# A key search that keeps its trial threshold, in a kernel whose order follows corrected durations

## The chip, the cores and the metric

The kernel runs on one core of a Trainium2 chip. Its engines are TensorE (PE; PEld is its weight load), VectorE (DVE), ScalarE (ACT), GpSimd (POOL) and SyncE (SP, which issues the transfers). The metric is the device time of one execution in microseconds (us). The trace is one profiled execution, which gives the span from the first to the last instruction and the granted TensorE clock.

## The reference

A decoder block on x of 2048 tokens by 1024 channels, in float32. After a norm and one input projection it has two branches. One is a state-space branch (S5, 32 groups of 64 complex states, solved over chunks of 8 tokens). The other is sparse attention: an indexer scores every earlier key for each query, the 256 best are kept, and eight heads attend to those.

```python
rel = jax.nn.relu(jnp.einsum('bqhd,bsd->bqhs', qib, kif))
iscore = jnp.einsum('bqhs,bqh->bqs', rel, wib * w_scale)
iscore = jnp.where(visible[None], iscore, -jnp.inf)
_, idx = lax.top_k(iscore, k_sel)          # k_sel = 256
...
merged = sigmoid(g_ssm) * (y_ssm @ w_proj_ssm) + sigmoid(g_att) * (y_att @ w_proj_attn)
x = x + merged @ w_out
h2 = rms(x)
x = x + (silu(h2 @ w_ffn_gate) * (h2 @ w_ffn_up)) @ w_ffn_down
```

Matrix products are done as three products of a high and a low part (`mm3`), so PE carries most of the work.

## The kernel before

**Streams.** After phase 1 (norm, input projection) three streams of work share the engines: `state` (the state-space branch), `attention` (the indexer's top-k and then the attention, in four rounds of four query tiles of 128), and `dense` (gates, then four blocks of 512 tokens: merge, output projection, norm, FFN). Block `tb` starts when the attention of its tiles is done (`attended >= 4 * (tb + 1)`), so the top-k and attention of a round run beside the dense block of the round before.

**The plan.** Each stream is a Python generator. While the program is built, `Pace` books every instruction on a model of its engine (`note`: a price from operation, size and type; the time when the engine, `free`, and the data, `done`, are ready). `among` and `pick` take the first stream whose next step could start by the time the model gives for PE; a step that waits on `idle("DVE")` may come when DVE's booked time is no more than `AHEAD` past PE's (2.5 us, 7 in the dense blocks). `spare` chooses by these prices between POOL, DVE and ACT for side work. The result is a fixed order on each engine's queue; at run time an engine takes its instructions in that order.

**The top-k.** `topk` (method of `Block`) first writes the scores of a tile into `S[i]` (128 queries by (i+1) x 128 keys), then `search` finds, for every query, the bits of the 256th largest score, from bit 30 to bit 0, counting in each step how many scores lie beyond a trial threshold. A round has two tiles searched alone as "wide" groups (one column of state each; the count is a Sign activation on ACT, `jka`) and one "narrow" group of two tiles (two columns; the counts are compare-and-add passes on DVE, `jkd`). A narrow group searches the upper 16 bits on `H`, the upper halves as bf16; at bit 15 it rebuilds `H` as 16-bit numbers and searches the lower 16 in float32, with `tf` as the trial and `kf` as the part found. The first round has one wide and one narrow group of one tile each, its tiles 0 and 1 needing no search. The searches of a round run as streams beside each other.

**A step before.** `b` holds the key found so far and `tr` the trial. When the count `cnt` is there, DVE does three one- or two-column operations: `acc = cnt <= threshold`, a predicated copy of `tr` into `b` where `acc` holds, and `tr = b xor bit`:

```python
nc.vector.tensor_tensor(acc, cnt, thr if wide and bit < 30 else thd, op=ALU.is_le)
nc.vector.copy_predicated(cur, acc, tf if low and bit < 15 else tr)
if not low:
    nc.vector.tensor_scalar(tr, b, 1 << bit, None, op0=ALU.bitwise_xor)
```

In the lower half of a narrow group the same three work on `kf` and `tf`, with an addition in the place of the xor. Then come the counts with the new trial. After the last bit the ties are settled and a bias tile (`fin`) is stored for the attention.

**Names in the rows.** All rows show line 199, the helper through which each instruction is recorded, so tiles tell them apart. `f` is a PSUM bank of the dense blocks; `act`, `ww`, `mg` are the merge's inputs, weights and result; the products `f<-ww,mg` (256 columns) are the output projection, `x<-f,x` its and the FFN's residual additions, `ss`, `rr`, `ha` the norm behind it; `f<-h,ww` and `f<-wd,at` are the FFN's up and down products, `t` and `at` what stands between them. `lg`, `pt`, `po` belong to the attention.

Of the kernel before, what the change touches and what calls it, by code (L numbers as in the profile page):

```python
# [12 lines left out]
F32 = mybir.dt.float32  # L13
F32R = mybir.dt.float32r
BF16 = mybir.dt.bfloat16
I32 = mybir.dt.int32
U16 = mybir.dt.uint16
AF = mybir.ActivationFunctionType
ALU = mybir.AluOpType
# [13 lines left out]
TOPK = 256  # L33
# [18 lines left out]
class Pace:  # L52
# [4 lines left out]
    TABLES = {AF.Exp: ("exp",), AF.Tanh: ("exp", "silu"), AF.Silu: ("silu",)}  # L57
    RATE = {"DVE": (1.05e-3, 0.07), "ACT": (0.84e-3, 0.06), "POOL": (2.06e-3, 0.07)}

# [12 lines left out]
    def note(self, eng, op, args, kw):  # L72
        aps = [z for z in (*args, *kw.values()) if isinstance(z, bass.AP)]
        out = kw.get("out", aps[0])
        names = [self.key(z) for z in aps]
        size = math.prod(out.shape[1:])
        if eng == "PE":
            if op == "transpose":
                cost = size * 0.85e-3
            else:  # L80
                cost = math.prod(aps[2].shape[1:]) * 0.422e-3 * (1 if aps[1].dtype == F32R else 4)
        elif eng == "SP":
            cost = out.shape[0] * size * mybir.dt.size(out.dtype) / 360e3
        else:
# [8 lines left out]
            if "accum_out" in kw:  # L93
                cost += 0.2 if eng == "ACT" else 0.07
            if op == "reciprocal":
                cost += size * 5 * r
            elif eng == "POOL" and "pow" in str(kw.get("op")):
                cost += 0.4 + size * 0.1
            elif eng == "POOL" and op == "memset":
                cost -= size * r * 0.6  # L100
# [258 lines left out]
class Block:  # L359
# [431 lines left out]
    def topk(self, st, groups, KL):  # L791
# [39 lines left out]
        for j, (tiles, wide) in enumerate(groups):  # L831
            for i in tiles:
                S[i] = sp.tile([128, (i + 1) * 128], F32, name=f"S{i}")
                yield from iscore(i, S[i], kis)
            n = len(tiles)
            b = qp.tile([128, n], I32, name=f"b{j}", bufs=1)
            nc.vector.memset(b, -1)
            states.append((tiles, b))
# [4 lines left out]
        def count(x, i, t, c):  # L843

            nc.vector.tensor_scalar(jkd[:, :(i + 1) * 128], x, t, 0.0, op0=ALU.is_lt, op1=ALU.add, accum_out=c)

        def search(j, tiles, b, wide):

            n = len(tiles)
            thr, thd, cnt, kf, tf = (qp.tile([128, n], F32, name=f"{m}{j}", bufs=1)
                                     for m in ("thr", "thd", "cnt", "kf", "tf"))
            tr, acc, top = (qp.tile([128, n], I32, name=f"{m}{j}", bufs=1) for m in ("tr", "acc", "top"))
            for q, i in enumerate(tiles):
                W = (i + 1) * 128
                nc.vector.memset(thd[:, q:q + 1], float(W - TOPK))
                if wide:
                    nc.vector.memset(thr[:, q:q + 1], float(W - 2 * TOPK + 1))  # L860
            t = tr.bitcast(F32)
            nc.vector.tensor_scalar(tr, b, -1, None, op0=ALU.bitwise_xor)
            for q, i in enumerate(tiles):
# [3 lines left out]
            if not wide:  # L867
                X = {}
                for i in tiles:
                    yield idle("DVE")  # L870
                    X[i] = sp.tile([128, (i + 1) * 128], BF16, name=f"H{i}")
                    nc.vector.tensor_copy(X[i], S[i].bitcast(BF16).rearrange("p (w a) -> p w a", a=2)[:, :, 1])

            for bit in range(30, -1, -1):
                if wide:
                    yield idle("DVE", cnt)
                low = not wide and bit < 16
                cur = kf if low and bit < 15 else b
                nc.vector.tensor_tensor(acc, cnt, thr if wide and bit < 30 else thd, op=ALU.is_le)
                nc.vector.copy_predicated(cur, acc, tf if low and bit < 15 else tr)  # L880
                if not low:
                    nc.vector.tensor_scalar(tr, b, 1 << bit, None, op0=ALU.bitwise_xor)
                elif bit == 15:

                    nc.vector.tensor_scalar(top, b, 65535, None, op0=ALU.bitwise_xor)
                    nc.vector.tensor_scalar(kf, b, 0.0, None, op0=ALU.is_ge)
                    sg = qp.tile([128, n], F32, name=f"sgn{j}", bufs=1)
                    of = qp.tile([128, n], F32, name=f"off{j}", bufs=1)
                    nc.vector.tensor_scalar(sg, kf, 2.0, -1.0, op0=ALU.mult, op1=ALU.add)
                    nc.vector.tensor_scalar(of, kf, -65535.0, 65535.0, op0=ALU.mult, op1=ALU.add)  # L890
                    for q, i in enumerate(tiles):
# [11 lines left out]
                        nc.vector.tensor_tensor(X[i], X[i], Z, op=ALU.max)  # L903
                    nc.vector.memset(kf, 0.0)
                    nc.vector.memset(tf, float(1 << bit))
                else:
                    nc.vector.tensor_scalar(tf, kf, float(1 << bit), None, op0=ALU.add)
                for q, i in enumerate(tiles):
# [6 lines left out]
            yield idle("DVE", cnt)  # L915
            nc.vector.tensor_tensor(acc, cnt, thr if wide else thd, op=ALU.is_le)
            nc.vector.copy_predicated(b if wide else kf, acc, tr if wide else tf)
            if not wide:
                nc.vector.tensor_copy(tr, kf)
                nc.vector.tensor_tensor(b, b, tr, op=ALU.bitwise_xor)  # L920
# [1054 lines left out]
```

## Time and profile before

| | |
|---|---|
| median of 3 runs | 3481.62 us (3478.7 to 3488.02) |
| the profiled execution | 3482.83 us, span 3480.7 us |
| mean granted PE clock | 0.963 |
| PE busy | 3187.9 us, 92% |
| DVE busy | 2187.6 us, 63%, 4674 instructions |
| ACT, POOL busy | 1258.2 us (36%), 732.0 us (21%) |

Busy shares are means over stages with different limits; the stretches between 393.8 us (the first trial) and 2565 us alternate between searches and attention. A wait names the engine whose signal came last. Idle time of an engine counts only where it ends in idle time of PE or delays the end. A granted clock of 1.00 is 2.4 GHz, the lower level is half of it.

### The profile page before, as it was taken

What the parts mean: (1) busy time and instruction counts of PE and PEld (TensorE: products, weight loads), DVE (VectorE), ACT (ScalarE), POOL (GpSimd) and SP (SyncE); (2) the same over time, 40 slices, a digit from 0 to 9 for tenths busy, and PEclk for the clock granted to TensorE, in tenths of its full rate; (3) what the DMA queues carried; (4) which work ended last, traced back from release to release, by engine and by line L of the source; (5) the groups of instructions that cost most, each with busy time, mean ns of one, the idle gap of its engine ahead of it and who ended that gap; (6) DMA issues with size and microseconds to landing.
All of it is one profiled execution on the core that took longest, in us unless ns stands there. A gap on an engine that the chain in (4) does not pass through costs nothing. (4 is left out here: it accounts for less than half of the span.)

```text
span 3480.7 us, 44710 instructions
## 1 busy us (share of the span) xinstructions
PE 3187.9 (92%) x16292; PEld 2692.5 (77%) x16292; DVE 2187.6 (63%) x4674; ACT 1258.2 (36%) x2186; POOL 732.0 (21%) x1016
## 2 busy tenths in 40 slices
PE   6999989888978999988879999979699999999999
PEld 5879767766756888766778888758588888798887
DVE  4555675567577566698786775996876666322222
ACT  3141444546532444455212444664124443110000
POOL 3323777762213312244100000001000000000000
PEclk8999999999988999999989999999899999999999
DMA  4833323443448854766845325347363232755544
GB/s 133 247 117 112 123 81 110 134 129 100 146 163 292 283 196 172 254 216 211 305 147 224 124 81 189 148 178 264 127 252 116 95 144 91 274 222 218 193 170 181
DMA packets 321531, 605.70 MB, mean 174 GB/s; under 512 B 52896, under 2 KB 205216, under 8 KB 290592
## 3 DMA queue, kind: packets, MB, share of 16 engines
q1 hardware_dynamic: 321312, 602.86, 49.6%
q8 instruction: 128, 2.10, 0.2%
q14 instruction: 91, 0.75, 0.1%
HBM read 434.71 MB, written 166.89 MB: 173 GB/s over the span
## 5 line engine op out<-in xcount | busy, mean ns | idle before, releaser
L199 PE MATMUL f<-h,ww 128*128 128x512 f32 (+1 forms) x4416 | 1012.5, 383 | 3.3 <-DVE x L199 2.0
L199 PEld LDWEIGHTS f<-h,ww 128*128 128x128 f32 x4416 | 798.2, 189 | 158.5 <-DVE x L199 2.4
L199 PE MATMUL f<-wd,at 128*128 128x512 f32 x2112 | 529.6, 403 | 60.0 <-ACT at L199 37.7
L199 PEld LDWEIGHTS f<-wd,at 128*128 128x128 f32 x2112 | 402.0, 194 | 156.3 <-issue 26.5
L199 PE MATMUL gps<-hT,gw 128*128 128x512 f32 x1536 | 386.9, 402 | 10.3 <-ACT gsg L199 9.8
L199 ACT ACTIVATE jka<-S,tr 128x896 bf16<-128x896 f32 (+6 forms) x217 | 305.6, 1408 | 234.6 <-DVE tr L199 170.2
L199 PEld LDWEIGHTS gps<-hT,gw 128*128 128x128 f32 x1536 | 285.6, 191 | 72.5 <-ACT gsg L199 9.5
L199 DVE TENSOR_TENSOR x<-f,x 128x512 f32<-128x512 f32 x352 | 236.5, 687 | 94.7 <-PE f L199 94.0
L199 PE MATMUL mm<-w,hT 128*128 128x512 f32 (+1 forms) x1152 | 283.4, 404 | 7.3 <-DVE hT L199 7.1
L199 DVE TENSOR_TENSOR tl<-pt,th 128x512 fp32r<-128x512 f32 (+1 forms) x288 | 184.2, 658 | 146.7 <-ACT th L199 145.9
L199 DVE SCALAR_TENSOR_TENSOR t<-t,f 128x512 f32<-128x512 f32 (+1 forms) x127 | 84.4, 665 | 305.2 <-PE f L199 260.7
L199 PEld LDWEIGHTS mm<-w,hT 128*128 128x128 f32 x1152 | 243.4, 241 | 33.2 <-DVE hT L199 8.8
L199 ACT CAST th<-pt 128x512 fp32r<-128x512 f32 (+1 forms) x288 | 155.8, 563 | 234.0 <-PE pt L199 232.1
L199 PE MATMUL f<-act,ww 128*128 128x512 f32 x768 | 188.2, 406 | 34.9 <-DMA act<-act 14.2
L199 POOL TENSOR_TENSOR g<-g,g 128x512 f32<-128x512 f32 x31 | 39.8, 1283 | 856.6 <-issue 553.4
L199 PEld LDWEIGHTS f<-act,ww 128*128 128x128 f32 x768 | 149.4, 197 | 73.3 <-issue 16.5
L199 PE MATMUL f<-ww,mg 128*128 128x256 f32 x1536 | 192.2, 288 | 10.5 <-DMA ww<-wc 4.1
L199 PEld LDWEIGHTS f<-ww,mg 128*128 128x128 f32 x1536 | 190.0, 196 | 13.1 <-issue 5.2
L199 ACT ACTIVATE P<-P,m 128x1024 f32<-128x1024 f32 (+7 forms) x192 | 172.2, 900 | 71.4 <-DVE m L199 71.1
L199 PE MATMUL lg<-kk,q 128*128 128x512 f32 (+1 forms) x640 | 183.2, 388 | 1.4 <-DMA kk<-kk 1.4
L199 ACT CAST at<-t 128x512 fp32r<-128x512 f32 (+1 forms) x92 | 55.2, 600 | 326.3 <-DVE t L199 326.3
L199 ACT ACTIVATE t<-f 128x512 f32<-128x512 f32 (+1 forms) x92 | 52.9, 575 | 310.8 <-PE f L199 310.7
(356 smaller groups left out, 4668.6 us busy)
## 6 DMA issues: line engine op xcount, KB each, us to landing
ww<-wc SPq DMA_DIRECT2D x180, 1024.0 KB, 4.9
wd<-wc SPq DMA_DIRECT2D x66, 1024.0 KB, 8.5
wc<-ww SPq DMA_DIRECT2D x60, 1024.0 KB, 7.4
raw<-in_w_in_dram SPq DMA_DIRECT2D x104, 256.0 KB, 3.3
wc<-wd SPq DMA_DIRECT2D x22, 1024.0 KB, 7.6
x<-in_x_dram SPq DMA_DIRECT2D x32, 512.0 KB, 5.8
gate<-gsg SPq DMA_DIRECT2D x64, 256.0 KB, 2.1
g<-gate SPq DMA_DIRECT2D x64, 256.0 KB, 5.5
```

What stands on the lines that cost most here:

```text
L199: return f(*args, **kw)
```

## The change

The search keeps the trial threshold itself in `tr` (or `tf`) and corrects it after each count. `missed` makes, in one operation, the word to take back: (count misses the target) times twice the bit, an integer in `un` or a negative float in `uf`. A second operation combines it with the trial and the next bit: two xors in one scalar-tensor-tensor instruction, or two additions. The copies, `acc`, `thr`, `thd` and `kf` go, and the memsets that fed them; `b` is made once, at bit 15 or at the end. The narrow count is now of scores at or above the trial instead of below it.

Beside it, prices of the plan change: POOL per element 2.06 to 2.25 ns; a product of PE from 0.422 ns a column to (columns + 32) / 2.4 GHz; a DVE operation with an accumulator 0.14 us more instead of 0.07; DVE operations of at most 8 columns get fixed prices (0.1 us for `tensor_scalar` and memset, 0.25 for a predicated copy, 0.2 for others); DVE operations on fewer than 128 partitions 0.09 more; POOL's power 0.15 us a column instead of 0.1.

```diff
--- before.py
+++ after.py
@@ -55,7 +55,7 @@
     AHEAD, SLACK, BIAS = 2.5, 0.3, 0.0
     TIGHT = 0.5
     TABLES = {AF.Exp: ("exp",), AF.Tanh: ("exp", "silu"), AF.Silu: ("silu",)}
-    RATE = {"DVE": (1.05e-3, 0.07), "ACT": (0.84e-3, 0.06), "POOL": (2.06e-3, 0.07)}
+    RATE = {"DVE": (1.05e-3, 0.07), "ACT": (0.84e-3, 0.06), "POOL": (2.25e-3, 0.07)}
 
     def __init__(self, nc):
         self.free = dict.fromkeys(("PE", "DVE", "ACT", "POOL", "SP"), 0.0)
@@ -78,7 +78,8 @@
             if op == "transpose":
                 cost = size * 0.85e-3
             else:
-                cost = math.prod(aps[2].shape[1:]) * 0.422e-3 * (1 if aps[1].dtype == F32R else 4)
+                n = math.prod(aps[2].shape[1:])
+                cost = (n + 32) / 2.4e3 if aps[1].dtype == F32R else n * 4 / 2.4e3
         elif eng == "SP":
             cost = out.shape[0] * size * mybir.dt.size(out.dtype) / 360e3
         else:
@@ -91,11 +92,17 @@
             elif eng == "DVE" and op in ("tensor_scalar", "tensor_tensor") and short:
                 cost -= size * r / 2
             if "accum_out" in kw:
-                cost += 0.2 if eng == "ACT" else 0.07
+                cost += 0.2 if eng == "ACT" else 0.14
             if op == "reciprocal":
                 cost += size * 5 * r
+            elif eng == "DVE" and size <= 8 and op not in ("tensor_scalar", "memset"):
+                cost = 0.25 if op == "copy_predicated" else 0.2
+            elif eng == "DVE" and size <= 8:
+                cost = 0.1
+            elif eng == "DVE" and out.shape[0] < 128:
+                cost += 0.09
             elif eng == "POOL" and "pow" in str(kw.get("op")):
-                cost += 0.4 + size * 0.1
+                cost += 0.4 + size * 0.15
             elif eng == "POOL" and op == "memset":
                 cost -= size * r * 0.6
             if eng == "ACT" and op == "activation":
@@ -834,7 +841,6 @@
                 yield from iscore(i, S[i], kis)
             n = len(tiles)
             b = qp.tile([128, n], I32, name=f"b{j}", bufs=1)
-            nc.vector.memset(b, -1)
             states.append((tiles, b))
         banks.close()
         self.spare_banks = 4
@@ -842,24 +848,19 @@
 
         def count(x, i, t, c):
 
-            nc.vector.tensor_scalar(jkd[:, :(i + 1) * 128], x, t, 0.0, op0=ALU.is_lt, op1=ALU.add, accum_out=c)
+            nc.vector.tensor_scalar(jkd[:, :(i + 1) * 128], x, t, 0.0, op0=ALU.is_ge, op1=ALU.add, accum_out=c)
 
         def search(j, tiles, b, wide):
 
 
 
 
+
             n = len(tiles)
-            thr, thd, cnt, kf, tf = (qp.tile([128, n], F32, name=f"{m}{j}", bufs=1)
-                                     for m in ("thr", "thd", "cnt", "kf", "tf"))
-            tr, acc, top = (qp.tile([128, n], I32, name=f"{m}{j}", bufs=1) for m in ("tr", "acc", "top"))
-            for q, i in enumerate(tiles):
-                W = (i + 1) * 128
-                nc.vector.memset(thd[:, q:q + 1], float(W - TOPK))
-                if wide:
-                    nc.vector.memset(thr[:, q:q + 1], float(W - 2 * TOPK + 1))
+            cnt, tf, uf = (qp.tile([128, n], F32, name=f"{m}{j}", bufs=1) for m in ("cnt", "tf", "uf"))
+            tr, un, top = (qp.tile([128, n], I32, name=f"{m}{j}", bufs=1) for m in ("tr", "un", "top"))
             t = tr.bitcast(F32)
-            nc.vector.tensor_scalar(tr, b, -1, None, op0=ALU.bitwise_xor)
+            nc.vector.memset(tr, 0)
             for q, i in enumerate(tiles):
                 yield idle("DVE")
                 count(S[i], i, t[:, q:q + 1], cnt[:, q:q + 1])
@@ -871,23 +872,34 @@
                     X[i] = sp.tile([128, (i + 1) * 128], BF16, name=f"H{i}")
                     nc.vector.tensor_copy(X[i], S[i].bitcast(BF16).rearrange("p (w a) -> p w a", a=2)[:, :, 1])
 
+            def missed(out, value, signs):
+
+                if signs:
+                    W = (tiles[0] + 1) * 128
+                    nc.vector.tensor_scalar(out, cnt, float(W - 2 * TOPK + 1), float(value), op0=ALU.is_gt, op1=ALU.mult)
+                else:
+                    nc.vector.tensor_scalar(out, cnt, float(TOPK), float(value), op0=ALU.is_lt, op1=ALU.mult)
+
             for bit in range(30, -1, -1):
                 if wide:
                     yield idle("DVE", cnt)
                 low = not wide and bit < 16
-                cur = kf if low and bit < 15 else b
-                nc.vector.tensor_tensor(acc, cnt, thr if wide and bit < 30 else thd, op=ALU.is_le)
-                nc.vector.copy_predicated(cur, acc, tf if low and bit < 15 else tr)
-                if not low:
-                    nc.vector.tensor_scalar(tr, b, 1 << bit, None, op0=ALU.bitwise_xor)
-                elif bit == 15:
+                if low and bit < 15:
+                    missed(uf, -(2 << bit), False)
+                    nc.vector.scalar_tensor_tensor(tf, uf, float(1 << bit), tf, op0=ALU.add, op1=ALU.add)
+                else:
+                    missed(un, -1 if bit == 30 else 2 << bit, wide and bit < 30)
+                    if not low:
+                        nc.vector.scalar_tensor_tensor(tr, un, 1 << bit, tr, op0=ALU.bitwise_xor, op1=ALU.bitwise_xor)
+                if low and bit == 15:
+                    nc.vector.tensor_tensor(b, tr, un, op=ALU.bitwise_xor)
 
                     nc.vector.tensor_scalar(top, b, 65535, None, op0=ALU.bitwise_xor)
-                    nc.vector.tensor_scalar(kf, b, 0.0, None, op0=ALU.is_ge)
+                    nc.vector.tensor_scalar(uf, b, 0.0, None, op0=ALU.is_ge)
                     sg = qp.tile([128, n], F32, name=f"sgn{j}", bufs=1)
                     of = qp.tile([128, n], F32, name=f"off{j}", bufs=1)
-                    nc.vector.tensor_scalar(sg, kf, 2.0, -1.0, op0=ALU.mult, op1=ALU.add)
-                    nc.vector.tensor_scalar(of, kf, -65535.0, 65535.0, op0=ALU.mult, op1=ALU.add)
+                    nc.vector.tensor_scalar(sg, uf, 2.0, -1.0, op0=ALU.mult, op1=ALU.add)
+                    nc.vector.tensor_scalar(of, uf, -65535.0, 65535.0, op0=ALU.mult, op1=ALU.add)
                     for q, i in enumerate(tiles):
                         c = slice(q, q + 1)
                         yield idle("DVE")
@@ -901,10 +913,7 @@
                         Z = jkd.bitcast(U16)[:, :W]
                         nc.vector.tensor_scalar(Z, S[i], top.bitcast(F32)[:, c], 65535.0, op0=ALU.is_gt, op1=ALU.mult)
                         nc.vector.tensor_tensor(X[i], X[i], Z, op=ALU.max)
-                    nc.vector.memset(kf, 0.0)
                     nc.vector.memset(tf, float(1 << bit))
-                else:
-                    nc.vector.tensor_scalar(tf, kf, float(1 << bit), None, op0=ALU.add)
                 for q, i in enumerate(tiles):
                     if wide:
                         nc.scalar.activation(jka[:, :(i + 1) * 128], S[i], AF.Sign, bias=t[:, q:q + 1], scale=-1.0,
@@ -913,10 +922,12 @@
                         yield idle("DVE")
                         count(X[i], i, (tf if low else t)[:, q:q + 1], cnt[:, q:q + 1])
             yield idle("DVE", cnt)
-            nc.vector.tensor_tensor(acc, cnt, thr if wide else thd, op=ALU.is_le)
-            nc.vector.copy_predicated(b if wide else kf, acc, tr if wide else tf)
-            if not wide:
-                nc.vector.tensor_copy(tr, kf)
+            if wide:
+                missed(un, 1, True)
+                nc.vector.tensor_tensor(b, tr, un, op=ALU.bitwise_xor)
+            else:
+                missed(uf, -1, False)
+                nc.vector.tensor_tensor(tr, tf, uf, op=ALU.add)
                 nc.vector.tensor_tensor(b, b, tr, op=ALU.bitwise_xor)
 
         yield from self.pace.among([search(j, *states[j], groups[j][1]) for j in range(len(groups))])
```

## Rows read from the trace of the kernel before

**Rows 1.** Stretches: us, busy PE, PEld, DVE, ACT, POOL (instructions), clock, DMA.

```profile
760.00:1120.00 360.00, 301.19 (x1488) 247.31 (x1489) 257.92 (x659) 165.86 (x297) 98.89 (x84) 0.92 0.50 163
...
1480.00:1840.00 360.00, 300.76 (x1468) 252.74 (x1467) 303.84 (x629) 134.75 (x185) 95.28 (x52) 0.91 0.62 224
1840.00:2200.00 360.00, 359.47 (x1936) 306.85 (x1935) 241.78 (x496) 154.53 (x292) 1.08 (x3) 1.00 0.38 139
2200.00:2560.00 360.00, 303.03 (x1516) 254.85 (x1516) 303.38 (x626) 163.33 (x185) 13.77 (x13) 0.93 0.52 193
```

**Rows 2.** PE's waits, 1480 to 1840: waiter, releaser, total us, times, longest.

```profile
PE f L199 <- ACT at L199: 24.6, 5, 8.0
PE f L199 <- DVE ss L199: 13.7, 1, 13.7
```

**Rows 3.** PE's waits, 2200 to 2560.

```profile
PE f L199 <- DVE ss L199: 25.1, 1, 25.1
PE f L199 <- ACT at L199: 11.5, 3, 10.2
PE f L199 <- DVE t L199: 10.1, 3, 4.3
```

**Rows 4.** Timeline, DVE and PE: start us, us, instruction [idle before <-releaser].

```profile
2459.78 2.08 DVE L199 TENSOR_SCALAR_CACHE_REDUCE jkd<-H,tf 128x1792 bf16<-128x1792 uint16 x1
...
2462.37 0.68 DVE L199 SCALAR_TENSOR_TENSOR x<-f,x 128x512 f32<-128x512 f32 x1
...
2466.58 1.94 PE L199 MATMUL f<-ident,ha 128*128 128x128 f32 x8 [25.05 <-DVE ss L199]
```

**Rows 5.** PE's waits, 760 to 1120.

```profile
PE f L199 <- DMA act<-act: 14.2, 1, 14.2
```

**Rows 6.** Timeline of DVE, a narrow step and a wide one.

```profile
2403.47 0.16 DVE L199 TENSOR_TENSOR acc<-cnt,thd 128x2 int32<-128x2 f32 x1
...
2404.06 1.95 DVE L199 TENSOR_SCALAR_CACHE_REDUCE jkd<-H,tf 128x1664 bf16<-128x1664 uint16 x1
...
2405.93 0.16 DVE L199 TENSOR_TENSOR acc<-cnt,thr 128x1 int32<-128x1 f32 x1
2406.12 0.22 DVE L199 COPY_PREDICATED_SCALAR b<-acc,tr 128x1 int32 x1
2406.38 0.15 DVE L199 TENSOR_SCALAR tr<-b 128x1 int32<-128x1 int32 x1
2406.45 2.07 DVE L199 TENSOR_SCALAR_CACHE_REDUCE jkd<-H,tf 128x1792 bf16<-128x1792 uint16 x1
```

**Rows 7.** Timeline of DVE, two small operations behind the search.

```profile
2501.76 0.16 DVE L199 TENSOR_TENSOR b<-b,tr 128x2 int32<-128x2 int32 x1
2501.84 2.34 DVE L199 TENSOR_SCALAR_CACHE_REDUCE jkd<-S,b 128x2048 bf16<-128x2048 f32 x1
...
2513.67 0.15 DVE L199 SCALAR_TENSOR_TENSOR r<-ssum,gt 128x1 f32<-128x1 f32 x1
```

**Rows 8.** All instructions on the compare's result: count: ns min/median/max, first and last, forms.

```profile
L199 DVE TENSOR_TENSOR acc<-cnt,thr x217: 146/153/2353, 398.6 to 2442.4; 128x1 int32<-128x1 f32 x109
L199 DVE TENSOR_TENSOR acc<-cnt,thd x135: 147/161/2386, 396.1 to 2501.2; 128x2 int32<-128x2 f32 x96, 128x1 int32<-128x1 f32 x39
```

**Rows 9.** Groups of DVE, 2200 to 2560: busy us, mean ns | idle before.

```profile
L199 DVE TENSOR_SCALAR_CACHE_REDUCE jkd<-H,tf 128x1792 bf16<-128x1792 uint16 x16 | 33.2, 2076 | 0.3
```

**Rows 10.** Timeline of PE, two runs of products.

```profile
2348.50 43.80 PE L199 MATMUL f<-act,ww 128*128 128x512 f32 x192 [1.33 <-DVE x L199]
...
2400.47 20.78 PE L199 MATMUL f<-ww,mg 128*128 128x256 f32 x171 [0.22 <-DVE mg L199]
```

**Rows 11.** DVE's waits, 2200 to 2560.

```profile
DVE mg L199 <- ACT mg L199: 19.9, 8, 3.6
```

**Rows 12.** Timeline, the end of the last attention: PE and the SP queue.

```profile
2971.16 1.11 PE L199 MATMUL lg<-r,hsel 8*128 8x128 f32 x8
...
3004.68 4.27 SPq L199 DMA_DIRECT2D act<-att  x4
```

## The prediction

> **What bounds the kernel now.** I read the table by stage first. TensorE (PE) is busy 92% of the span, so the question is where the other 8% sits. [rows 1] is a table of stretches: in the attention stretch shown, 1840 to 2200, PE has 359.5 of 360 us and a granted clock of 1.00. Nothing can be won there. In the three stretches in which a key search runs it has 301, 301 and 303 of 360 us, at a mean clock of 0.92, 0.91 and 0.93. So each search stretch loses 57 to 59 us of idle PE, and about 0.07 to 0.09 x 360 = 25 to 32 us more because part of it ran at the lower of the two clock levels. That is some 85 us a stretch, 255 us in all, and it is all that this change can reach.
>
> Then the waits of PE in these stretches. In the third and fourth searches they name the dense block's own short chains: `at` and `t` (the gated products of the FFN) and `ss`, the norm's sum [rows 2, 3]. These are cheap operations; what makes them late must be read off VectorE's (DVE's) queue. [rows 4] shows it at the longest wait: PE sits idle 25.05 us before 2466.58, while DVE runs count after count of the search; the last residual addition `x<-f,x` before the norm, 0.68 us of work, comes at 2462.37, behind them, and `ss` only after it. DVE works in the order in which the build-time plan issued, and the plan believed that it would be through earlier. The second search stretch is different: its longest wait, 14.2 us, is for a transfer at the start of the first dense block [rows 5].
>
> **Removed work, by rows.** A wide step (one column) is compare, predicated copy, xor: the compare starts at 2405.93, the xor at 2406.38 and the next DVE instruction at 2406.45, 0.52 us after the compare [rows 6]. A narrow one (two columns) starts at 2403.47 and its count at 2404.06: 0.59. The new step is a compare with multiply, then a scalar-tensor-tensor that depends on it. From a one-column operation to the one that depends on it the row has 0.19 us (compare to copy) [rows 6]; a one-column scalar-tensor-tensor takes 0.15, no longer than a compare, and after a two-column xor of two tensors the next instruction starts 0.08 later [rows 7]. So I take 0.27 for a wide step and 0.39 for a narrow one whose count must wait: 0.25 and 0.20 saved. No row shows an integer scalar-tensor-tensor with two xors. Its bounds are those 0.08 (like the plain xor) and the 0.25 us of the predicated copy (2406.12 to 2406.38); then a wide step saves only 0.07 and a narrow one about 0.03. I take the first, since the operation is nearest to the xor in kind and to the row of [rows 7] in length.
>
> The compares number 217 + 135 = 352 [rows 8], which is 224 wide steps and 128 narrow ones. 224 x 0.25 + 128 x 0.20 = 82 us of DVE, by the other bound 224 x 0.07 + 128 x 0.03 = 20 us. A search of two wide groups (64 steps) and one narrow (32) saves 22 us, the first search (one and one) 14. The removed set-up memsets are one-column and some three dozen: with the reset of `b`, 2 us in all, which I leave out. Count operations change from less-than to at-least, same form and cost. Some compares take up to 2353 ns instead of 153 [rows 8]; what holds them can hold the new operations as well, so I count no gain there.
>
> **The corrected prices move the order.** The plan lets a search step in when DVE, by its own prices, is at most AHEAD = 7 us past PE. Per stage of two wide groups and one narrow: (a) an old step was priced 3 x 0.07 = 0.21 us and takes 0.52 or 0.59; a new one is priced 0.1 + 0.2 = 0.30 and takes 0.27 or 0.39. Unpriced DVE time falls from 64 x 0.31 + 31 x 0.38 = 32 us to about 1. (b) A count of the narrow group is priced at half its columns, (1792 x 1.05 / 2) ns + 0.14 = 1.08 us, and takes 2.08 [rows 9]. The diff leaves the halving and adds 0.07: of about 60 us unpriced in the last search (31 counts at 1792, 31 at 1664), 56 stay. (c) PE: a 512-column product was priced 0.216 us and takes 43.80 / 192 = 0.228; a 256-column one 0.108 against 20.78 / 171 = 0.1215 [rows 10]. The new 0.227 and 0.120 are right. But the low price had worked against (a) and (b): by 5% of some 278 us (303 less 25 for the clock) it held back 14 us of DVE work a stage; now 2.
>
> So lateness that the plan does not see was, in the last search, 32 + 60 - 14 = 78 us and becomes 1 + 56 - 2 = 55: relief 23 us a stage, nearly what the steps save.
>
> The Trainium skill speaks against (c): TensorE: Matmul & The Clock Gate, Back-to-back issue gap, gives an isolated warm 512-column product about 215.7 ns. By it the old price was right and the new one 5% too slow; [rows 10] measures 228 ns, so the row decides. It matters for the second rival alone.
>
> **The sum.** The waits of the last search that DVE's lateness can explain are 25.1 + 11.5 + 10.1 us in [rows 3], 47 of 57 us. If they shrink in proportion, 23 / 78 of 47 is 14 us; if one for one, 23. I take 20 for the last search and 20 for the third, whose DVE is as full (304 of 360 us [rows 1]). For the second search 8, since much of its idle time is transfers and weight splitting; for the first, short one, 3: 51 us of idle PE. The lower clock has cost half as much as the idle time in these stretches (25 to 57, 32 to 59), so half of 51 again, 25. The sum is 76 us. Other price changes (GpSimd 9% dearer, DVE under 128 partitions, ScalarE untouched) only reshuffle the order; I cost them at nothing, since the attention stretch has no idle PE to lose or win [rows 1]; should they disturb a good order elsewhere, I allow 10 us either way inside the range. From the profiled run's 3482.8 us (span 3480.7 and 2.1 around it; the median of the runs is 3481.6): about **3407 us**. Bounds: with 0.25 us for the new operation the relief is some 6 us a stage and the gain 20 to 25 (3460); with one-for-one waits in three searches, 69 + 10 + half of it, 118 (3364).
>
> **Rivals.**
> *The time saved was hidden.* DVE idles 57 us in each of the last two search stretches too [rows 1], 19.9 us of it in the last one for ScalarE's share of the merge, which stands in ScalarE's queue beside the wide steps [rows 11]. Where the search is not the last thing PE waits for, a shorter step gives longer idle time. Then only part of the 25.1 and 13.7 us boundary waits shrinks, 20 us with 10 of clock: 3452. For it: that row. Against: in [rows 4] DVE is the one that is late.
> *Slower: the new PE price crowds the blocks.* With PE priced slower, 5% (12% in the 256-column stretch ahead of a norm) more DVE work, with counts still at half price, is put between the same products: 12 us of lateness more a stage. This decides only if the 31 us relief of (a) falls in DVE's idle slots: more than 60% of it would have to. Then three stages x 12 us x 47/78 is 22 us idle, half again for the clock: 33 us, 3515. Should the skill's 215.7 ns hold, this would be the likelier way.
> *Slower, lesser: attention slips.* The last attention product starts at 2971.16 and block 3's load of its result at 3004.68 [rows 12], a margin of 33 us. A search spread over more PE work than that leaves PE without filler. Since the new prices of DVE and PE rise together, I expect a slip under 10 us.
> *More than said.* Both norm waits vanish and the clock stays up: 3340 to 3364.
>
> **How the numbers follow.** A measurement here tells 0.3%, 10 us, from no change. Forecast, 3364 to 3442: 0.60. Hidden, 3442 to 3471: 0.15. More than said: 0.05. No change within 10 us: 0.08. Slower: 0.12 (crowding 0.09, slip 0.03). Faster is 0.80. The range 3360 to 3482 leaves out the slower case, half of the unchanged one at most and most of the last: 0.8 held.
>
> **What the profile after would show.** Right: no predicated copies in the search, about 352 compare-multiplies and as many second steps, 0.27 us from the first's start to what follows in a wide step; search stretches with 20 us less idle PE each and a clock above 0.95; the waits on `ss` and `at` shorter; attention stretches still full. Wrong: the double xor at 0.25 us or more; waits on `ss` as long as before though the steps are shorter (hidden); longer waits with more counts between the 256-column products (crowding); or PE idle between 2960 and 3010 for attention (slip). The halved price of counts is what I trust least: lateness left at 55 us a stage could bunch up before one norm.

## The result, and the profile after

The changed kernel takes 3463.1 us (median of 4 runs, 3459.7 to 3467.8) against 3483.6 for the one before (4 runs, 3478.7 to 3488.0). The ratio is 0.9939, 95% interval 0.9927 to 0.9951. So the gain is 20 us, where 76 were forecast. The profiled execution took 3462.8 us: span 3460.6, mean granted clock 0.965.

The page's busy times of the kernel after (its rows show line 206, where the helper that records the instructions stands in it):

```profile
PE 3201.6 (93%) x16292; PEld 2698.5 (78%) x16292; DVE 2133.6 (62%) x4306; ACT 1261.8 (36%) x2187; POOL 706.1 (20%) x1003
```

VectorE (DVE) has 368 instructions less and 54 us less busy time. First, the steps themselves, on the timeline of DVE after: a wide step, then a narrow one with the count behind it (columns: start, duration, both us).

```profile
2181.06 0.15 DVE L206 TENSOR_SCALAR un<-cnt 128x1 int32<-128x1 f32 x1
2181.24 0.16 DVE L206 SCALAR_TENSOR_TENSOR tr<-un,tr 128x1 int32<-128x1 int32 x1
2181.32 0.15 DVE L206 TENSOR_SCALAR un<-cnt 128x1 int32<-128x1 f32 x1
...
2404.15 0.17 DVE L206 TENSOR_SCALAR uf<-cnt 128x2 f32<-128x2 f32 x1
2404.36 0.16 DVE L206 SCALAR_TENSOR_TENSOR tf<-uf,tf 128x2 f32<-128x2 f32 x1
2404.55 1.95 DVE L206 TENSOR_SCALAR_CACHE_REDUCE jkd<-H,tf 128x1664 bf16<-128x1664 uint16 x1
```

From 2181.06 to 2181.32 is 0.26 us for a wide step, from 2404.15 to 2404.55 is 0.40 for a narrow one: as forecast (0.27, 0.39). The operation with two xors behaves like the plain xor: what follows starts 0.08 us after it.

The same four stretches as in [rows 1], after:

```profile
760.00:1120.00 360.00, 301.30 (x1480) 245.93 (x1478) 246.17 (x561) 162.44 (x286) 89.20 (x68) 0.92 0.52 168
1480.00:1840.00 360.00, 312.69 (x1526) 262.63 (x1527) 289.34 (x530) 125.62 (x174) 92.49 (x49) 0.93 0.68 245
1840.00:2200.00 360.00, 355.95 (x1911) 302.43 (x1910) 257.78 (x532) 176.69 (x312) 1.18 (x4) 1.00 0.35 126
2200.00:2560.00 360.00, 321.88 (x1609) 273.31 (x1608) 280.28 (x508) 149.07 (x179) 13.47 (x12) 0.94 0.57 213
```

As everything behind a gain comes earlier, fixed stretches no longer hold whole searches, so here is the trace cut from the first count of each search to the last store of its bias tiles, before and then after:

```profile
394.70:519.90 125.20, 106.45 (x486) 83.43 (x485) 102.26 (x351) 54.64 (x127) 98.67 (x235) 0.95 0.28 81
786.70:1130.00 343.30, 286.51 (x1449) 237.07 (x1448) 245.63 (x632) 149.62 (x270) 93.20 (x67) 0.93 0.54 176
1487.50:1854.90 367.40, 308.16 (x1497) 258.77 (x1496) 309.25 (x636) 133.04 (x182) 91.51 (x50) 0.91 0.60 216
2205.00:2570.40 365.40, 308.43 (x1537) 259.18 (x1536) 309.07 (x625) 161.34 (x182) 13.67 (x13) 0.93 0.52 192
```

```profile
386.40:502.20 115.80, 106.11 (x484) 83.31 (x483) 95.11 (x295) 54.51 (x126) 93.86 (x233) 0.94 0.31 88
791.60:1104.40 312.80, 256.41 (x1215) 207.62 (x1214) 211.95 (x511) 143.37 (x257) 80.79 (x58) 0.91 0.53 172
1449.70:1810.20 360.50, 309.25 (x1501) 258.95 (x1500) 302.94 (x538) 134.00 (x182) 109.97 (x58) 0.92 0.65 231
2162.50:2504.70 342.20, 301.60 (x1489) 255.16 (x1488) 288.06 (x522) 161.56 (x182) 13.71 (x13) 0.94 0.55 203
```

In those pieces TensorE (PE) idle (length less busy time) before and after is: first search 18.7 and 9.7 us, second 56.8 and 56.4, third 59.2 and 51.3, fourth 57.0 and 40.6. The forecast had 3, 8, 20 and 20 us less; it became 9, 0, 8 and 16. The mean clock in them is 0.91 to 0.95 before and 0.91 to 0.94 after.

Over the span, PE's idle time fell from 292.8 to 259.0 us. The busy time lost because the granted clock stood at the lower of the two levels (1.2 instead of 2.4 GHz) did not fall with it: by the trace's records of the clock it went from 73.4 to 81.5. The rest of PE's busy time, taken at full clock, is 3114 and 3120 us for the same 16292 products; I did not follow these 6 us. So the 20 us are 34 us less idle time, less 8 of clock and 6 of busy time.

What PE waited for in the third search (1450 to 1803) and the fourth (2162 to 2492), after (us in total, times, longest):

```profile
PE f L206 <- ACT at L206: 21.2, 4, 15.5
PE f L206 <- DVE wd L206: 9.4, 4, 2.6
PE f L206 <- DVE un L206: 6.9, 3, 3.5
```

```profile
PE f L206 <- ACT at L206: 9.1, 1, 9.1
PE f L206 <- DVE t L206: 7.1, 4, 2.4
PE f L206 <- DVE x L206: 6.6, 3, 4.5
PE f L206 <- DVE h L206: 6.3, 2, 5.9
...
PE f L206 <- DVE ss L206: 3.9, 1, 3.9
```

The wait of 25.1 us on the norm's sum `ss` [rows 3] has become one of 3.9, but others of the same kind have grown beside it. The longest in the third search is on `at`, and its row names ScalarE (ACT). The timeline shows that DVE is behind it:

```profile
1656.45 1.40 DVE L206 TENSOR_SCALAR_CACHE_REDUCE jkd<-H,tf 128x1152 bf16<-128x1152 uint16 x1
...
1668.22 1.54 DVE L206 TENSOR_SCALAR_CACHE_REDUCE jkd<-H,tf 128x1280 bf16<-128x1280 uint16 x1
...
1670.09 0.69 DVE L206 SCALAR_TENSOR_TENSOR t<-t,f 128x512 f32<-128x512 f32 x1
1671.46 0.69 DVE L206 TENSOR_TENSOR at<-t,at 128x512 fp32r<-128x512 f32 x1 [0.69 <-ACT at L206]
1671.48 0.80 PE L206 MATMUL f<-wd,at 128*128 128x512 f32 x1 [15.52 <-ACT at L206]
```

Between 1656.45 and 1669.8 DVE runs eight counts of the narrow group in a row (1.4 and 1.5 us each), and the gated product `t<-t,f`, 0.69 us of work, stands behind them. ACT can round it only then, and PE had been idle for 15.5 us. It is the picture of [rows 4] at another place: counts bunch up on DVE ahead of one short chain.

### The profile page after: what moved, and what is told of

Read it like the earlier page. It is cut to its first block, busy times and chain, and to the rows that moved or that the text cites. A ratio compares the mean times of both kernels' runs of the same rounds, so it can differ in the third digit from the quotient of the medians.

```text
span 3460.6 us, 44348 instructions
## 1 busy us (share of the span) xinstructions
PE 3201.6 (93%) x16292; PEld 2698.5 (78%) x16292; DVE 2133.6 (62%) x4306; ACT 1261.8 (36%) x2187; POOL 706.1 (20%) x1003
## 5 line engine op out<-in xcount | busy, mean ns | idle before, releaser
L206 ACT ACTIVATE jka<-S,tr 128x1024 bf16<-128x1024 f32 (+6 forms) x217 | 305.6, 1408 | 172.4 <-DVE tr L206 127.0
L206 PEld LDWEIGHTS gps<-hT,gw 128*128 128x128 f32 x1536 | 287.9, 192 | 81.5 <-ACT gsg L206 17.3
```

The lines of the kernel that those rows point to most:

```text
L206: return f(*args, **kw)
```

## The experiments

Fifteen kernels ran, in four groups; each was timed beside the kernel before on the same chip, and the ratio is to that. The theories that the expectations number are my readings as they changed from group to group. `Pace` is the class that holds the plan's prices.

**First: steps and prices apart.**

e1: the new steps with the whole old `Pace`.

> The new two-operation step, with all prices of the plan as before. Theory 1 (a shorter step by itself takes DVE time out of PE's waits; corrected prices add what relief is left): 8 to 14 us faster than before, the rest of the 20 us of the whole change coming from the prices. Rival (the order decides, DVE's saved 60 us are hidden): within 5 us of before.

Measured: 3486.0 us, ratio 0.9998 (0.9987 to 1.0009). The new steps alone, 82 us of DVE work shorter by the rows, gain nothing, where theory 1 had 8 to 14 us.

e2: the old steps with the new `Pace`.

> The old three-operation step, with the new prices. Theory 1: 5 to 12 us faster than before, since each step is now priced at 0.55 us against 0.52 measured, where 0.21 stood. Rival (order decides): all of the 20 us is here. Rival (the new PE price crowds): slower than before by up to 15 us.

Measured: 3471.6 us, 0.9964 (0.9950 to 0.9978): some 13 us faster. (The text adds up the prices alone; with the waits explained below, this plan books an old step at 0.85 us.)

e3: the changed kernel, but a count is booked at its full length:

```diff
-            elif eng == "DVE" and op in ("tensor_scalar", "tensor_tensor") and short:
+            elif eng == "DVE" and op in ("tensor_scalar", "tensor_tensor") and short and "accum_out" not in kw:
```

> The changed kernel, with the narrow group's counts priced at all their columns (1.88 + 0.21 us for 1792 columns, where 1.15 stands and 2.08 is measured). Theory 1 (the waits that are left come from DVE work the plan books at half price): 10 to 30 us faster than the changed kernel, with the 15.5 us wait before 1671 and the 9.1 us wait before 2325 gone or under 4 us. Rival (PE's waits there are set by ScalarE or by the blocks' own chains): within 5 us of it. Rival (search drawn out, attention late): slower, with idle PE ahead of the last block.

Measured: 3415.8 us, 0.9804 (0.9788 to 0.9821). This one condition gains more than twice what the whole change did, and more than theory 1 had. Of its fourth search (2186 to 2562), the waits on the two tiles that were longest before:

```profile
PE f L206 <- DVE ss L206: 7.5, 1, 7.5
...
PE f L206 <- ACT at L206: 2.7, 1, 2.7
```

e4: the changed kernel with the old price of matmuls.

```diff
-                cost = (n + 32) / 2.4e3 if aps[1].dtype == F32R else n * 4 / 2.4e3
+                cost = n * 0.422e-3 * (1 if aps[1].dtype == F32R else 4)
```

> The changed kernel, with PE's products priced at 0.422 ns a column as before. Theory of crowding (the right PE price takes back relief by admitting 5 to 12% more DVE work per product): 8 to 20 us faster than the changed kernel. Theory 1 counts this as 12 us of lateness a stage against 31 of relief, so it expects the same sign but 5 to 15 us. Rival (PE's price does not matter): within 4 us.

Measured: 3457.5 us, 0.9915 (0.9899 to 0.9931). The corrected PE price costs some 6 to 8 us here; the intervals just touch. That is the low end of theory 1's 5 to 15.

e1 broke my reading: with the old step underpriced by 0.31 us, as I had it, the shorter step could not have gained nothing. I had to read `note` again. It adds 0.15 us after each result before an operation that depends on it may start, on DVE for DVE's own results too:

```python
after = [d for d in after if d and (d[1] != eng or eng in ("SP", "DVE", "POOL"))]
...
t = max([self.free[eng]] + [d[0] for d in after])
...
    self.free[eng] = t = t + cost
    d = (t + 0.15, eng)
```

An old step is a chain of three: it was booked at 0.21 + 2 x 0.15 = 0.51 us and took 0.52 [rows 6]. It was booked right. In e1 the new step is booked at 0.07 + 0.15 + 0.07 = 0.29, right again. So there was no step lateness to relieve, and the plan used each saved quarter of a microsecond to place the next step earlier: its last attention product comes at 2868 us, 104 us earlier than before. PE does idle 17 us less in e1 than before (275.7 against 292.8), but the clock takes 20 (93.4 against 73.4).

**Second: how much unseen work.** My theory became that one number counts, U, the DVE work of a search that the plan does not see, net of what a wrong PE price hides. For the last search, from prices and rows: a narrow bit takes 1.99 + 2.12 (counts with what follows them) + 0.59 = 4.70 us before and was booked at 1.01 + 1.08 + 0.15 + 0.51 + 0.15 = 2.90. 31 bits of that are 56 us; the low PE price hides 14: U is 42. After: 4.51 against 2.98 is 47, less 64 wide steps booked 0.19 too long (0.1 + 0.15 + 0.2 = 0.45 for 0.26), less 2 for PE: 33.

f1: old steps, new `Pace`, counts at full length.

> The old three-operation step with the new prices and the counts at their full price. Theory 1 now reads: what PE loses in the search follows from the DVE work that the plan books too low, so nearly all of the gain of the full count price is there with the old step too, and the step's own 75 us of DVE then stretch the search: 5 to 20 us slower than the same prices with the new step (3421 to 3436). Rival (the saved DVE time is worth its length once the order is right): 40 us slower or more, 3456 and above. Rival (the step is worth nothing): within 4 us of 3416.

Measured: 3485.6 us, 1.0008 (0.9998 to 1.0018), 50 us above theory 1's range and in that of the rival that the shorter step is worth its length. But U is not that of e3; it is about -39: the plan now books an old step at 0.85 us, as its three operations are 0.2 + 0.25 + 0.1 and two waits. Two stretches of f1, the fourth search (2317 to 2725) and what comes after it, then the main wait in the second:

```profile
2317.00:2725.00 408.00, 391.87 (x1896) 332.01 (x1895) 320.02 (x644) 170.15 (x196) 3.17 (x4) 0.98 0.51 193
2725.00:3012.00 287.00, 230.09 (x1264) 180.52 (x1264) 199.97 (x450) 141.13 (x267) 0.00 (x0) 0.90 0.13 45
```

```profile
PE lg L206 <- DMA kk<-kk: 15.0, 3, 13.4
```

The search now costs PE only 16 us, but lasts 408 us instead of some 356. By its end too little dense work is left, the last attention runs without filler (PE busy 230 of 287 us, clock 0.90), and the last block starts when attention ends. Part of the loss is paid there; how much of it is overpricing and how much the longer step itself, f1 can't tell.

f2: e1 with 0.07 us more on the new step's second operation. (The text takes the old step's booking as 0.21, as the prediction did; with the waits it is 0.51, and this kernel's is 0.36.)

> The new two-operation step in before's plan, each step booked at the 0.21 us that the old one had, so that the order stays as near to before's as it can. Prediction's direct term (DVE time taken out of PE's waits at an unchanged order, relief of about 22 us a stage): 15 to 40 us faster than before. Rival (hidden: the order decides when DVE works): within 6 us of before.

Measured: 3481.3 us, 0.9988 (0.9979 to 0.9998). The 15 to 40 us of the prediction's direct term did not come.

f3 and f4: the changed kernel with counts at 75% and 125% of their length.

```diff
-                cost -= size * r / 2
+                cost -= size * r / (4 if "accum_out" in kw else 2)               # f3
+                cost += size * r * (0.25 if "accum_out" in kw else -0.5)         # f4
```

> The changed kernel with the narrow counts booked at three quarters of their columns, half the error of 56 us that is left in the last search. Theory 1 (time follows the unbooked DVE work): between the changed kernel and the full price, 3434 to 3446. Rival (the full price won by luck of one order): anywhere else, with no step between.

> The changed kernel with the narrow counts booked at one and a quarter of their columns, more than they take. Theory 1: nothing left to win, within 8 us of the full price (3408 to 3424), the search drawn out by some 30 us. Rival (dearer counts help by giving the dense blocks the right of way): 10 us faster than the full price or more. Rival (search drawn out, attention late): 10 us slower or more, with idle PE ahead of the last block.

Measured: 3428.8 us, 0.9845 (0.9832 to 0.9859), and 3443.9 us, 0.9887 (0.9874 to 0.9901). f3 is faster than expected; f4 misses theory 1 by 20 us and fits the rival of a search drawn out. With 50% and 100% (3463 and 3416) that is a bowl with its floor near the true length.

**Third: is it the order, or the work?** g1: e1 with counts at full length. g2: e3 with the old PE price.

> The new step with before's prices, but the narrow counts booked at all their columns. Theory 2 (the shorter step shortens the search and so widens the margin between the last attention product and the last block; right prices of the counts spend that margin on shorter waits; the other prices matter little): 3410 to 3435, with the last attention product less than 25 us before the last block's first. Rival (all new prices are needed): above 3445.

> The changed kernel with the counts at full price and PE's products at the old price of 0.422 ns a column. With nothing else booked too low, the low PE price makes the search longer in PE's terms. Theory 2: the margin before the last block is used up already, so 5 to 25 us slower than the full count price alone (3421 to 3441), lost after the last search. Rival (crowding by the right PE price, as with the half-priced counts): 5 to 10 us faster.

Measured: g1 3415.0 us, 0.9798 (0.9785 to 0.9812); g2 3448.8 us, 0.9894 (0.9880 to 0.9907), 8 us beyond theory 2's range. With counts booked right, the other price corrections add nothing (g1 and e3 agree). The old PE price, 6 us better in e4, is 33 us worse here: its sign depends on what else is wrong.

g3 and g4: after and e3, with the step's first operation issued three times more. The repeats write the same values again and go past the plan, so every queue keeps its order.

```diff
+                for v in (nc.vector, nc.vector.eng, nc.vector.eng, nc.vector.eng):
+                    v.tensor_scalar(out, cnt, at_least, ...)
 ...
```

> The changed kernel, each step's compare written three more times by instructions that the plan does not book: every queue keeps its order, and DVE has 352 x 3 more one- and two-column operations, some 75 us by 0.07 us each. Theory 2 (DVE time of the steps is hidden at this order, it only moves the last attention towards the last block, 84 us of margin): within 12 us of the changed kernel, the last attention product some 30 to 60 us later. Theory 1 (DVE time goes into PE's waits one for one): 30 us slower or more.

> The full count price with the same unbooked extra operations: 75 us more DVE at its order, whose margin before the last block is about nothing. Theory 2: the time shows, 25 us slower than the full count price or more, since PE's waits in the search return (the search is full of DVE work) and nothing is left to hide behind. Rival (step time is hidden at any order): within 10 us of 3416.

Measured: g3 3629.2 us, 1.0416 (1.0402 to 1.0431); g4 3560.5 us, 1.0212 (1.0197 to 1.0227). A wide step of g3 on the timeline:

```profile
2292.97 0.15 DVE L206 TENSOR_SCALAR un<-cnt 128x1 int32<-128x1 f32 x1
2293.15 0.53 DVE L878 TENSOR_SCALAR un<-cnt 128x1 int32<-128x1 f32 x3
2293.72 0.16 DVE L206 SCALAR_TENSOR_TENSOR tr<-un,tr 128x1 int32<-128x1 int32 x1
```

2292.97 to 2293.72 is 0.75 us instead of 0.18, and a narrow one grows by 0.61, so 224 x 0.57 + 128 x 0.61 = 206 us more DVE work (not the 75 of the expectation), and 166 us (145 in g4) more time than without the repeats. Theory 2, by which g3 would have stayed within 12 us, is refuted. In a fixed order DVE work in a search is not hidden: it costs 0.7 to 0.8 us per us.

**Fourth: the saving itself, in the old order.** h1: the kernel before, in which the three old operations are only booked and the two new ones issued past the plan; the order on PE, ACT, POOL and SP is that of before, instruction for instruction.

```diff
-                nc.vector.tensor_tensor(acc, cnt, thr if wide and bit < 30 else thd, op=ALU.is_le)
-                nc.vector.copy_predicated(cur, acc, tf if low and bit < 15 else tr)
+                book("tensor_tensor", acc, cnt, thr if wide and bit < 30 else thd)
+                book("copy_predicated", cur, acc, tf if low and bit < 15 else tr)
 ...
+                    missed(un, ...)
 ...
+                        raw.scalar_tensor_tensor(tr, un, 1 << bit, tr, op0=ALU.bitwise_xor, op1=ALU.bitwise_xor)
```

> Before's plan and order on every queue, to the instruction (the old three operations are booked and not issued, the new two are issued and not booked). DVE's steps are 0.26 and 0.19 us shorter than booked, 22 us less in the last search. Theory 3 (PE's waits follow the DVE work that the plan does not see, and the step, whose chain of three the plan booked at 0.51 us, was not among it; a shorter step pays only as far as the plan does not book it shorter): 20 to 45 us faster than before, 3438 to 3463. Rival (the saved DVE time is hidden behind other waits at any order): within 6 us of before.

Measured: 3428.1 us, 0.9835 (0.9822 to 0.9849): 57 us gained, for 82 us of DVE work saved by the rows, 0.7 per us; more than the 20 to 45 of theory 3.

h2: after, with one unbooked repeat per step in place of g3's three.

> The changed kernel at its own order, each step with one more unbooked one- or two-column operation of 0.19 us, which makes it nearly as long as the old step; 67 us of DVE in all. Theory 3, by the three operations that cost 166 us for 206 us of DVE: 40 to 60 us slower than the changed kernel, 3503 to 3523. Rival (the first tens of us are absorbed by idle time of DVE, only more than that shows): less than 20 us slower.

Measured: 3509.4 us, 1.0063 (1.0049 to 1.0076). 352 x 0.19 = 67 us more work, 46 us more time: 0.7 again.

h3: e3, with the new step's second operation booked at 0.02, so that the step is booked as measured (0.1 + 0.15 + 0.02 = 0.27).

```diff
-                cost = 0.25 if op == "copy_predicated" else 0.2
+                cost = 0.25 if op == "copy_predicated" else 0.02 if op == "scalar_tensor_tensor" else 0.2
```

> The changed kernel with the counts at full price and the new step booked at 0.1 + 0.15 + 0.02 = 0.27 us, as measured, where the prices of the change make 0.45. The plan then books the search within some 6 us of what it takes. Theory 3: as fast as the full count price alone, 3408 to 3425, with the search shorter in the plan and 15 us or more between the last attention product and the last block, which there was none of. Rival (overbooking the step is itself a gain): 3430 or more.

Measured: 3416.0 us, 0.9804 (0.9789 to 0.9819), the same as e3. What differs is the margin at the end. The rows are the last index product of attention and the first product of the last block's merge, on PE's timeline, in e1, e3 and h3:

```profile
2867.33 1.10 PE L199 MATMUL lg<-r,hsel 8*128 8x128 f32 x8
...
3018.09 2.20 PE L199 MATMUL f<-act,ww 128*128 128x512 f32 x9
```

```profile
2947.98 2.07 PE L206 MATMUL lg<-r,hsel 8*128 8x128 f32 x8 [1.28 <-DVE r L206]
2949.98 3.35 PE L206 MATMUL f<-act,ww 128*128 128x512 f32 x7
```

```profile
2897.56 1.10 PE L206 MATMUL lg<-r,hsel 8*128 8x128 f32 x8
...
2949.05 2.20 PE L206 MATMUL f<-act,ww 128*128 128x512 f32 x9
```

The margin between them is 150 us in e1, none in e3, some 50 in h3; before it was 41, after the change 83. So e3 and h3 take the same time with and without a margin.

All kernels with the new step by U of the last search (an estimate from the plan's prices and the rows, as above), with the time:

| new step | U, us | time, us | | new step | U, us | time, us |
|---|---|---|---|---|---|---|
| h2 (one repeat) | 51 | 3509 | | f3 | 5 | 3429 |
| e1 | 41 | 3486 | | h3 | -6 | 3416 |
| f2 | 34 | 3481 | | g1 | -16 | 3415 |
| after | 33 | 3463 | | e3 | -23 | 3416 |
| e4 | 21 | 3457 | | g2 | -35 | 3449 |
| h1 | 20 | 3428 | | f4 | -51 | 3444 |
| g3 (three repeats) | 89 | 3629 | | g4 (three repeats) | 32 | 3561 |

With the old step: before 42, 3484; e2 18, 3472; f1 -39, 3486. Among the kernels without repeats it is a bowl: the more work is unseen, the longer PE waits (over the span it idles 276 us in e1 and 228 in e3); work booked but not there draws the searches out (f1). The floor lies between -6 and -23. The order along it is not perfect: h1 is 29 us faster than e4 at the same U.

And U is not all. g4 has the U of the changed kernel and is 97 us slower; it holds 206 us more DVE work. At about equal U the old, longer step is slower too, by 15 to 44 us near 20 (e2 against e4 and h1) and by some 40 near -40 (f1 against g2 and f4), though by nothing at 42 (before against e1). So the time follows the amount of DVE work as well as the part of it that the plan does not see; between kernels of equal work U tells the direction and roughly the size, not the last 30 us.

## Why the prediction was right and wrong

**Right: the durations.** The new steps cost what [rows 6, 7] said, 0.26 and 0.40 us. DVE is what PE's norm and gate waits hang on, and its steps are not hidden work: h1, h2, g3 and g4 show 0.7 to 0.8 us per us with the order held still. The rival "hidden" is refuted by h1: 57 us gained, with 82 saved. That the measured 3463 us lies in the stretch given to it (3442 to 3471) is chance.

**Wrong: step (a) of the price changes,** "an old step was priced 3 x 0.07 = 0.21 us and takes 0.52 or 0.59". The prices are right, but the plan's booking of a chain includes its waits of 0.15 us, so it was 0.51 us, not 0.21. So the "32 us to about 1" of unseen step time was never there, and the relief of 23 us a stage shrinks to 9: what is left of it is that the new step is booked longer than it is (0.45 for 0.26), and that against 12 us of PE compensation. h1 and e1 show what that is worth. Both issue the new step under the prices of before; h1 books it as the old one (0.51 us, relief 22 by the same working) and gains 57 us, e1 books it as itself (0.29, relief 1) and gains nothing. What the plan books as saved, the order gives away again. The change gains 37 us less than h1. That the booking of the step is all of this is not shown: e4 has the U of h1 and is 29 us slower, and each of these kernels has an order of its own. Nor is e1's nothing all missing relief, since its 17 us of idle time went to the clock.

**Wrong too, and by the terms of the sum the larger miss: the clock term.** I gave each us of idle time saved half a us of clock on top, 25 in the sum; the clock took 8 instead. Of the 56 us missing, 33 are this term, 17 are idle time (34 of 51) and 6 PE's busy time at full clock. In h1 idle fell by 51 us (292.8 to 241.6), as much as the sum had, and the loss to the clock went only from 73.4 to 71.2. The lower level itself lasted 258 us before and 241 after, but PE idled through 111 us of it before and 78 after. So by this count nearly all of the idle time saved lay at the lower level, and PE now works at half speed there. Why the granted clock stayed low stays open; I made no run for it. These are single traces, and the mean clock of the kernel before ranges from 0.959 to 0.965 over its runs, so a few us of this are not shown.

**(b), the halved count price,** was rightly what I trusted least. The 56 us that the change leaves unseen were the largest part of the account: booking the counts right (e3) gains 47 us more.

**(c), the PE price.** The compensation of 14 us that becomes 2 was right in kind: taking the price back gives 6 to 8 us (e4) while U is positive and costs 33 (g2) when it is negative. As a rival, "crowding", it was true at a fraction of its 33 us and did not decide.

**Attention slips:** not by under 10 us, but the other way. Before, the margin ahead of the last block was 41 us between the two products named above; after, it is 83 (2912.4 to 2995.7), and in e1 150. The searches became denser, so attention ended earlier. The slip is real where DVE is overbooked (f1). But no margin is no loss by itself: it is gone in e3 and g1, the fastest, as in g2 and f4, whose time I didn't follow to its rows.

**By stage,** the third search kept most of its loss: it gained 8 us of 20, and the second nothing of 8. The bunching at 1671 (15.5 us) stands in the third; and in that search the step's second operation took 628 ns on average instead of 159 (below), which I had said it could. That is no loss against before, though: the compare took 457 there.

## What to carry to other kernels

When a build-time plan sets the order, add up a chain as the plan books it, waits included, before calling it underpriced; ask of each saved microsecond whether the plan books it too, because then it places the next piece earlier and the lateness can stay (e1 against h1). Account for all unbooked work of the bottleneck's supplier together: correcting one price can lose time while a larger error of the other sign stands beside it, and the largest (here the halved counts, 47 us in e3 and 71 from e1 to g1) should be mended first. To tell work from order on the chip, change the work past the plan, so that every queue stays as it was, and measure the exchange rate.

## What the runs showed of the hardware

Small DVE operations with two tensor inputs often stretch while GpSimd (POOL) is at work. The new step's second operation in the third search, where POOL splits weights, and in the fourth, where it hardly does; groups of instructions, busy us, mean ns | idle before:

```profile
L206 DVE SCALAR_TENSOR_TENSOR tr<-un,tr 128x1 int32<-128x1 int32 x62 | 38.9, 628 | 2.1
```

```profile
L206 DVE SCALAR_TENSOR_TENSOR tr<-un,tr 128x1 int32<-128x1 int32 x62 | 9.9, 159 | 2.1
```

One case on the timeline of POOL and DVE, with a 4.74 us pair on POOL:

```profile
1645.59 4.74 POOL L206 TENSOR_TENSOR wd<-raw,wd 128x1024 fp32r<-128x1024 f32 x2 [5.09 <-ACT wd L206]
```

```profile
1646.68 1.33 DVE L206 TENSOR_SCALAR uf<-cnt 128x2 f32<-128x2 f32 x1
1648.04 2.30 DVE L206 SCALAR_TENSOR_TENSOR tf<-uf,tf 128x2 f32<-128x2 f32 x1
```

The first of these two ends with the first instruction of the pair (at 1648.0), the second at 1650.34 with the whole pair (1650.33). That is the rule in both traces: all 53 second operations of the step that take over 0.3 us, and all 46 such compares of the kernel before, end 0.01 to 0.02 us behind the end of an instruction of POOL. So they wait for it to end.

Over the whole trace the one-column operation takes 741 ns on average when POOL is busy at its start (71 times) and 159 when it isn't (161 times). The compare of before did the same [rows 8], 593 against 153, but one-column compares with a constant (147 both ways) and one-column predicated copies (217 both ways) do not; two-column ones can, as the 1.33 us above. The Trainium skill, GPSIMD Engine Reference, section Specifications, says that GpSimd's SBUF interface is shared with VectorE, with contention for instructions that have two SBUF inputs or run in a mode that uses two ports. The traces agree for the scalar-tensor-tensor and the compare of two tensors and put the price at up to 2.3 us for an operation of 0.16; the one-column predicated copy, which reads two tiles as well, is not hit. So the change did not remove this stall (a mean of 457 ns for the compare in the third search before, 628 after): it moved from the first operation of a step to the second.
